# Six plain column blocks, late sums of squares, and new ranks and slacks for the list scheduler of a two-layer encoder

## The chip, the cores and the metric

The kernel runs on one core of a Trainium2 chip. The metric is the device time of one execution in microseconds (us). The core has a matrix engine (TensorE, PE; PEld is its weight load), VectorE (DVE), ScalarE (ACT), GpSimd (POOL), a queue (SP) that issues DMAs, an on-chip memory SBUF and accumulation banks PSUM.

## What is computed

Two layers of an encoder over 512 positions of width 1024, all in float32. Each layer:

```
h = rmsnorm(x, g_attn);  proj = h @ w_in
group A: windowed attention (8 q heads, 2 kv heads, dim 64, sinks)
group B: differential attention (4 heads): softmax 1 - lambda * softmax 2
x = x + concat(A, B) @ w_out
h = rmsnorm(x, g_ffn)
gate, val = split(h @ w_up)           # 22 column blocks of 128 each
gate = depthwise conv of width 3 over positions
x = x + (silu(gate) * val) @ w_down
```

## The kernel before

Every product is made of three float32r products of a high and a low part (hi*hi, hi*lo, lo*hi), so each weight tile `wr` that a DMA brings is split: ScalarE casts it to `wh`, VectorE (in some cases GpSimd) subtracts to get `wl`. The tiles `wr`, `wh` and `wl` have 2, 3 and 3 buffers.

**A layer** has a front and a mixer. The front is the first product `akv`/`aq`, seven projections `pj_...`, attention A (scores `sc_a`, softmax `so_a`, transposes `pt_a` into the one PSUM bank of tag `at`, their copies `p_a`, values `pv_a`), attention B (`sc_b`, `e_b`, transposes `wt_b`, values `yb`, their norm with `ss_yb`, `rr_yb`, `rt_yb`) and the output projection `wo` in three passes. The last pass adds its two halves of 256 positions to the residual `x`; after the second half the norm of the mixer is begun for each of the 8 row blocks k (`Norm.add`): ScalarE writes `nf_h` (x times the gain), VectorE `nf_l` (the rest). The squares (`Norm.squares`: `nf_q` on ScalarE, summed into `nf_sum` on VectorE) go to TensorE as `nf_ss`, then through GpSimd to the row factor `nf_r`, which TensorE spreads (`rps`) and ScalarE copies to `rb`. The factor multiplies the products afterwards, so the first products of the mixer need only `nf_h` and `nf_l`.

**The mixer** has 22 column blocks f. A plain block (`up_step`) is two products, gate and value, of 8 row blocks x 3 matmuls of 512 columns. A pair (`pair_step`, `up_pair`) makes two blocks together in a fast form with seven products of half size for each of gate and value (4 row blocks x 3 matmuls of 256 columns each). It needs sums of the weights (`ws`, four for each of gate and value, `w_sums`), splits of four weight tiles instead of two, sums of its inputs (`mixer_forms`: `fa`, `fb`, `fc`, `f`), and sums of its products (`dp`, `du`, `gp`). In a pair the last product T4 goes into the bank of T3, after VectorE has read T3 into `du` (`fourth`). With `PLAIN = 4`, blocks 0 to 3 are plain and 9 pairs follow. The down-projection `dn` of one part of blocks (`FF_PARTS`) stands between the pairs of the next. `gp` also is the padded gate, and `cv` its convolution.

**The order of all work is set when the program is built**, by a list scheduler (`Machine`). Each strand of work is a generator (a track) that yields one operation at a time, with a rank from the table `RK` (lower goes first). `Machine.run` takes for each engine the operations that could start within a hold (`HOLD`, 0.02 for PE) of the earliest, and of these the one of the lowest rank; it estimates when inputs are ready from modelled durations plus a slack per reading engine (`NEAR`, in us). Where an operation may go to VectorE or GpSimd (`either`), it takes the one that would end first, with `BIAS` added to VectorE:

```
q, op = min(((self.when(v), v) for v in (t[3] if isinstance(t[3], tuple) else (t[3],))),
            key=lambda v: self.begin(v[1], v[0]) + v[1].pitch + (BIAS if v[1].eng == "DVE" else 0))
```

The ranks that matter below: `nsq` (squares of the mixer's norm), `xl` (the adds of the last `wo` pass and the `Norm.add` behind them), `w` and `wf` (splits of weights), `sum` (`ws`), `hf` (forms), `sec` (`du`), `evac` (copies of projections out of PSUM), `a` and `b` (attention). The chip's engines each run their list in order; the estimates have no part in the run.

Of the kernel before, what the change touches and what calls it, by code (L numbers as in the profile page):

```python
# [14 lines left out]
ALU = mybir.AluOpType  # L15
# [3 lines left out]
S = 512  # L19
# [7 lines left out]
EPS = 1e-6  # L27
NEG = -1e30
FF_PARTS = ((0, 6), (6, 12), (12, 18), (18, 22))
PLAIN = 4  # L30
CHUNKS = ("akv", "aq0", "aq1", "bv0", "bk1", "bk0", "bq0", "bq1", "bv1")
CW = 256
RP = 4
SMP = 12
FIRST_TAGS = ("mm", "sc")
AQ_TAGS = ("mm", "sc")
HOLD = 0.1
SWITCH = {True: 0.2, False: 0.085}
NEAR = {"PE": 0.053, "POOL": 0.079, "DVE": 0.06, "ACT": 0.035}
BIAS = 0  # L40
SQ_FROM = 4
LO_CUT = 1
N_COL = NK + NK + 3 * NF + NF + 1
N_ROW = 4 * HD + 8 + 4 * HD


RK = {"w": (2, 45, 30), "qkb": (55, 18), "x": 33, "xl": 8, "a": 2, "b": 18, "evac": 49, "qka": 60, "kv": 45,
      "bn": 2, "nsq": 6, "av": -4, "bv": 4, "ch": 50, "add": 42, "sec": 1, "nxs": 42, "fin": 42, "sum": 25,
      "hf": 22, "wf": 36}


class Op:
# [101 lines left out]
class Machine:  # L154
# [52 lines left out]
    def when(self, op):  # L207
        t = self.free[op.eng]
        near = NEAR.get(op.eng, 0.035)
        for kind, items in (("r", op.reads), ("w", op.writes)):  # L210
# [50 lines left out]
    def run(self):  # L261
        while self.tracks:
            best = {}
            for t in list(self.tracks):
                while callable(t[3]) and t in self.tracks and t[3]():
                    self.step(t)
                if t not in self.tracks or callable(t[3]):
                    continue
                q, op = min(((self.when(v), v) for v in (t[3] if isinstance(t[3], tuple) else (t[3],))),
                            key=lambda v: self.begin(v[1], v[0]) + v[1].pitch + (BIAS if v[1].eng == "DVE" else 0))  # L270
                best.setdefault(op.eng, []).append((self.begin(op, q), t[0](), t[1], t, op, q))
# [5 lines left out]
            for eng, c in best.items():  # L277
                s0 = min(v[0] for v in c)
                hold = 0.02 if eng == "PE" else HOLD
                w = min((v for v in c if v[0] <= s0 + hold), key=lambda v: (v[1], v[2]))  # L280
# [21 lines left out]
def kernel(  # L302
# [20 lines left out]
    pe, dve, act, pool, sync = (Queue(e) for e in ("PE", "DVE", "ACT", "POOL", "SP"))  # L323
# [15 lines left out]
    def new(tag, name, shape=None, dtype=None):  # L339
        bufs, shp, dt = TAGS[tag]  # L340
        return m.got(tag, (ps if tag in BANKS else sb).tile(shape or shp, dtype or dt, tag=tag, bufs=bufs, name=name))
# [33 lines left out]
    def mixer_order():  # L375

        ups = [[(f, 1) for f in range(f0, min(f1, PLAIN))] + [(f, 2) for f in range(max(f0, PLAIN), f1, 2)]
               for f0, f1 in FF_PARTS]
        for f, n in ups[0]:
            yield "up", 0, f, n  # L380
        for pi in range(len(FF_PARTS)):
            after = ups[pi + 1] if pi + 1 < len(FF_PARTS) else []
            at = {NK * i // len(after): u for i, u in enumerate(after)}
            for d in range(NK):
                if d in at:
                    yield ("up", pi + 1, *at[d])
                yield "dn", pi, d, 0
# [26 lines left out]
    def w_rank():  # L414
        i = state["used"]
        if i < len(units) and units[i][2] in ("up", "pair", "sum", "rest", "down") and len(ready) > i:
            return RK["wf"]
        return RK["w"][min(len(ready) - i, 2)]

# [36 lines left out]
    def w_sums():  # L456
        either = lambda *a: tuple(e.tensor_tensor(out=a[0], in0=a[1], in1=a[2], op=a[3]) for e in (dve, pool))
        for i in range(len(units)):
            if units[i][2] != "pair":
                continue  # L460
            yield lambda: i in pairs
            ra, rb = pairs.pop(i)
            nh = units[i][1][0] // 2
            a11, a12, a21, a22 = ra.tile[:, :nh], ra.tile[:, nh:], rb.tile[:, :nh], rb.tile[:, nh:]
            new_t = lambda j, r: Shared("prob", new("prob", f"ws{i}_{j}", [P, 2 * nh, P], F32), r)
            yield m.room("prob")
            s14 = new_t(0, 1)
            yield either(s14.tile[:, :nh], a21, a22, ALU.add)
            yield m.room("prob")
            s32 = new_t(1, 2)  # L470
            yield either(s32.tile[:, nh:], s14.tile[:, :nh], a11, ALU.subtract)
            yield either(s14.tile[:, nh:], a12, s32.tile[:, nh:], ALU.subtract)
            s32.done()
            raws[i + 1] = s14
            yield either(s32.tile[:, :nh], a11, a21, ALU.subtract)
            raws[i + 2] = s32
            ra.done()
            raws[i + 3] = rb
# [55 lines left out]
    class Norm:  # L534
# [16 lines left out]
            m.flags.add(f"{self.name}{k}")  # L551

        def squares(self):
            eng = dve
            for k in range(NK):
                yield m.has(f"{self.name}{k}")
                if k == 0:
                    yield m.room("tab")
                    self.part = new("tab", f"{self.name}_sum", [P, S])
                    yield act.activation(self.part, x_sb[k], AF.Square)  # L560
                    continue
                yield m.room("tmp")
                sq = new("tmp", f"{self.name}_q{k}")
                yield act.activation(sq[:, :S], x_sb[k], AF.Square)
                yield eng.tensor_tensor(out=self.part, in0=self.part, in1=sq[:, :S], op=ALU.add)
                m.drop("tmp", sq)
            m.flags.add(f"{self.name}_sq")

# [21 lines left out]
    def loads():  # L590
# [11 lines left out]
        for f in (w_load, w_high, w_low):  # L602
            m.spawn(w_rank, f(4))
        m.spawn(lambda: RK["sum"], w_sums())
        yield lambda: len(his) >= 5
# [59 lines left out]
    def layer(l, norm):  # L665
# [73 lines left out]
        def qk_track(nm, views, gone, tp, tab, dst, rq, rank, is_kv=False):  # L739
            def go():  # L740
                yield m.has(f"{h_in.name}_r")
                yield m.room("rp", 2)
                raw = new("rp", f"raw_{nm}{l}_{tp}")
                sq_t = new("rp", f"sq_{nm}{l}_{tp}")
                for i in range(2):
                    yield act.activation(raw[:, i], views[i], AF.Copy,
                                         scale=h_in.r[:, 2 * tp + i:2 * tp + i + 1])
                    gone(i)
                m.spawn(rank, qk_out(nm, raw, sq_t, tp, tab, dst, rq, is_kv))
            m.spawn(RK["evac"], go())  # L750

# [78 lines left out]
        def first_done(banks, tp):  # L830
            left = [2, 2]

            def gone(i):
                left[i] -= 1
                if not left[i]:
                    m.drop(*banks[i][:2])
            qk_track("ka", [b[2][:, :CW] for b in banks], gone, tp, 1, [v.unsqueeze(1) for v in ka], None, RK["kv"], True)
            qk_track("qa0", [b[2][:, CW:] for b in banks], gone, tp, 0, qa[0], rqa_of(0, tp), RK["qka"])

# [688 lines left out]
        def ffn():  # L1528
            steps = list(mixer_order())
            b_st["rb_left"] = PLAIN + 1  # L1530
            mix["forms"] = 14
# [149 lines left out]
```

## Time and profile before

| | |
|---|---|
| runs without the profiler | 1184.47 us median of 3 (1183.8, 1184.47, 1187.16) |
| the profiled execution, its own time | 1185.19 us |
| its span, first to last instruction | 1183.1 us |
| mean granted clock of TensorE | 0.993 |
| busy: TensorE, VectorE, ScalarE, GpSimd | 98%, 83%, 56%, 17% of the span |
| fronts | 0 to about 236 us (layer 0), about 592 to 823 us (layer 1) |
| mixers | about 236 to 592 us and 823 to 1183 us |

The span is 2.1 us shorter than the execution's own time. Matmuls overlap, so TensorE's busy time says little of how dense it is; the distance from one matmul's start to the next does.

### The profile page before, as it was taken

How to read it: one execution, taken by the hardware profiler on the slowest of the kernel's cores; microseconds unless marked ns; L12 is line 12 of the kernel's file. 1: busy time of each engine (PE TensorE's matmuls, PEld its weight loads, DVE VectorE, ACT ScalarE, POOL GpSimd, SP SyncE). 2: the span in 40 equal slices, each digit the busy share in tenths (PEclk: the TensorE clock that was granted, in tenths of full speed). 3: DMA queues.
4: the chain of work that ended last, by engine and by line, in shares of the span. 5: the costliest groups of instructions: out<-in, count | busy, mean ns of one | idle time of the engine just before them, and what ended most of it. 6: DMA issues, size and time to landing. Idle time of an engine off the chain costs nothing.

```text
span 1183.1 us, 20177 instructions
## 1 busy us (share of the span) xinstructions
PE 1163.1 (98%) x7796; PEld 1053.0 (89%) x7796; DVE 981.9 (83%) x1797; ACT 663.2 (56%) x1187; POOL 202.3 (17%) x254
## 2 busy tenths in 40 slices
PE   9999999999999999999999989999999999999998
PEld 7999888978999999999889989888789999999997
DVE  6988899779998888887659888898799988888863
ACT  6779766455564454444537876665555544544441
POOL 2433721010100000000042556110111000000000
PEclk9999999989999999999999999999899999999999
DMA  6221111123223322332332121111232223233323
GB/s 233 66 72 55 54 55 36 54 72 107 68 99 112 111 99 99 112 125 71 107 118 73 37 71 37 55 54 54 71 124 61 96 88 112 98 112 103 121 81 116
DMA packets 33343, 103.12 MB, mean 87 GB/s; under 512 B 3936, under 2 KB 4192, under 8 KB 33248
## 3 DMA queue, kind: packets, MB, share of 16 engines
q1 hardware_dynamic: 33248, 101.84, 26.0%
q8 instruction: 61, 1.00, 0.4%
q14 instruction: 34, 0.28, 0.1%
HBM read 99.73 MB, written 2.10 MB: 86 GB/s over the span
## 4 chain that ended last, share of the span: by engine, by line
PE 79%; DVE 13%; ACT 5%; issue 2%; POOL 0%; DMA 0%; SPq 0%; DVEq 0%; ACTq 0%
PE up L258 32%; PE dn L258 20%; PE wo L258 6%; PE pj_bk L258 3%; PE pj_bv L258 2%; PE pj_akq L258 2%; PE pj_bq L258 2%; DVE wl L258 2%; PE yb L258 2%; PE sc_b L258 2%; PE pt_a L258 1%; PE pv_a L258 1%; PE sc_a L258 1%; PE wt_b L258 1%; ACT so_a L258 1%
## 5 line engine op out<-in xcount | busy, mean ns | idle before, releaser
L258 ACT CAST wh<-wr 128x1024 fp32r<-128x1024 f32 (+2 forms) x200 | 177.2, 887 | 158.9 <-PE up L258 41.3
L258 DVE TENSOR_TENSOR wl<-wr,wh 128x1024 fp32r<-128x1024 f32 (+2 forms) x193 | 196.7, 1020 | 62.9 <-ACT wh L258 62.7
L258 ACT CAST wh<-ws 128x1024 fp32r<-128x1024 f32 x72 | 75.4, 1048 | 109.2 <-DVE ws L258 46.1
L258 PE MATMUL up<-fc,wh 128*128 128x256 f32 x576 | 106.4, 285 | 1.8 <-DVE du L258 1.8
L258 PE MATMUL up<-fa,wh 128*128 128x256 f32 x576 | 107.0, 283 | 0.0
L258 PE MATMUL up<-fb,wh 128*128 128x256 f32 x576 | 105.6, 284 | 0.0
L258 PEld LDWEIGHTS up<-fc,wh 128*128 128x128 f32 x576 | 89.4, 191 | 2.6 <-ACT cv L258 2.1
L258 PEld LDWEIGHTS up<-fb,wh 128*128 128x128 f32 x576 | 89.8, 192 | 0.4 <-ACT dp L258 0.2
L258 PEld LDWEIGHTS up<-fa,wh 128*128 128x128 f32 x576 | 89.8, 192 | 0.1
L258 DVE TENSOR_TENSOR wl<-ws,wh 128x1024 fp32r<-128x1024 f32 x72 | 89.5, 1245 | 0.4 <-ACT wh L258 0.2
L258 PE MATMUL dn<-act,wh 128*128 128x512 f32 x288 | 88.9, 390 | 0.0
L258 PE MATMUL up<-fa,wl 128*128 128x256 f32 x288 | 81.7, 284 | 0.0
L258 PE MATMUL up<-fb,wl 128*128 128x256 f32 x288 | 81.5, 283 | 0.0
L258 PE MATMUL up<-fc,wl 128*128 128x256 f32 x288 | 81.4, 283 | 0.0
L258 PE MATMUL dn<-acth,wh 128*128 128x512 f32 x208 | 81.0, 389 | 0.0
L258 PE MATMUL dn<-actl,wh 128*128 128x512 f32 x208 | 81.0, 389 | 0.0
L258 PE MATMUL dn<-acth,wl 128*128 128x512 f32 x208 | 80.9, 389 | 0.0
L258 POOL TENSOR_TENSOR du<-du 128x256 f32<-128x256 f32 x12 | 8.9, 742 | 395.9 <-DVE du L258 395.9
L258 DVE TENSOR_TENSOR x<-x,dn 128x512 f32<-128x512 f32 x64 | 43.7, 682 | 32.8 <-PE dn L258 32.8
L258 DVE SCALAR_TENSOR_TENSOR cv<-gp,cols,cv 128x512 f32<-128x512 f32 x88 | 63.9, 745 | 0.0
L258 PEld LDWEIGHTS dn<-act,wh 128*128 128x128 f32 x288 | 53.3, 188 | 10.4
L258 ACT ACTIVATE e_b<-sc_b,mx_b,rqb 128x512 f32<-128x512 f32 x64 | 49.1, 776 | 14.6 <-DVE mx_b L258 14.6
(269 smaller groups left out, 3452.4 us busy)
## 6 DMA issues: line engine op xcount, KB each, us to landing
wr<-w_up SPq DMA_DIRECT2D x88, 512.0 KB, 4.5
wr<-w_down SPq DMA_DIRECT2D x48, 384.0 KB, 3.1
wr<-w_in SPq DMA_DIRECT2D x28, 512.0 KB, 3.5
wr<-w_out SPq DMA_DIRECT2D x16, 512.0 KB, 3.4
wr<-w_down SPq DMA_DIRECT2D x16, 256.0 KB, 2.6
x<-xT SPq DMA_DIRECT2D x8, 256.0 KB, 5.5
prob_f<-w_first SPq DMA_DIRECT2D x8, 256.0 KB, 5.6
wr<-w_first SPq DMA_DIRECT2D x4, 512.0 KB, 3.6
```

The lines of the kernel that those rows point to most:

```text
L258: getattr(self.raw[op.eng], op.name)(*op.args, **op.kw)
```

## The change

The number of plain blocks goes from 4 to 6, so each layer has 8 pairs instead of 9 and the first pair is blocks 6 and 7. The slack of TensorE's inputs goes from 0.053 to 0.15 us, that of ScalarE from 0.035 to 0.06, the hold of the other engines from 0.1 to 0.05, and `BIAS` from 0 to 0.3. Nearly all ranks change. The variable `eng` in `squares` is only renamed. No loop or formula of the computation is touched.

```diff
-PLAIN = 4
+PLAIN = 6
...
-HOLD = 0.1
+HOLD = 0.05
 SWITCH = {True: 0.2, False: 0.085}
-NEAR = {"PE": 0.053, "POOL": 0.079, "DVE": 0.06, "ACT": 0.035}
-BIAS = 0
+NEAR = {"PE": 0.15, "POOL": 0.079, "DVE": 0.06, "ACT": 0.06}
+BIAS = 0.3
...
-RK = {"w": (2, 45, 30), "qkb": (55, 18), "x": 33, "xl": 8, "a": 2, "b": 18, "evac": 49, "qka": 60, "kv": 45,
-      "bn": 2, "nsq": 6, "av": -4, "bv": 4, "ch": 50, "add": 42, "sec": 1, "nxs": 42, "fin": 42, "sum": 25,
-      "hf": 22, "wf": 36}
+RK = {"w": (2, 39, 1), "qkb": (55, 18), "x": 10, "xl": 28, "a": 12, "b": 18, "evac": 45, "qka": 400, "kv": 60,
+      "bn": 0, "nsq": 30, "av": -2, "bv": -2, "ch": 50, "add": 4, "sec": 400, "nxs": 18, "fin": 400, "sum": 2,
+      "hf": 10, "wf": 33}
```

**First place.** VectorE's order before, where layer 0's mixer begins: the last adds `x` of the output projection, the low parts `nf0_l2` to `nf0_l6` of the norm, and the running sum of squares `nf0_sum`.

```order
L258 SCALAR_TENSOR_TENSOR nf0_l2_3082<-x2_68,cols_75,nf0_h2_3064 128x512
L258 TENSOR_TENSOR wl27_3068<-wr27_2873,wh27_3052 128x1024
L258 SCALAR_TENSOR_TENSOR nf0_l3_3094<-x3_69,cols_75,nf0_h3_3078 128x512
L258 TENSOR_TENSOR nf0_sum_3044<-nf0_sum_3044,nf0_q2_3098 128x512
L258 SCALAR_TENSOR_TENSOR nf0_l4_3119<-x4_70,cols_75,nf0_h4_3085 128x512
L258 TENSOR_TENSOR nf0_sum_3044<-nf0_sum_3044,nf0_q3_3121 128x512
L258 SCALAR_TENSOR_TENSOR nf0_l5_3128<-x5_71,cols_75,nf0_h5_3091 128x512
L258 TENSOR_TENSOR nf0_sum_3044<-nf0_sum_3044,nf0_q4_3130 128x512
L258 TENSOR_TENSOR x6_72<-x6_72,wo0_2_1_6_3074 128x256
L258 TENSOR_TENSOR nf0_sum_3044<-nf0_sum_3044,nf0_q5_3137 128x512
L258 TENSOR_TENSOR x7_73<-x7_73,wo0_2_1_7_3087 128x256
L258 SCALAR_TENSOR_TENSOR nf0_l6_3146<-x6_72,cols_75,nf0_h6_3143 128x512
```

The same place in the changed kernel:

```order
L258 SCALAR_TENSOR_TENSOR nf0_l2_3062<-x2_68,cols_75,nf0_h2_3054 128x512
L258 TENSOR_TENSOR x4_70<-x4_70,wo0_2_1_4_3050 128x256
L258 TENSOR_TENSOR x5_71<-x5_71,wo0_2_1_5_3065 128x256
L258 SCALAR_TENSOR_TENSOR nf0_l3_3080<-x3_69,cols_75,nf0_h3_3070 128x512
L258 TENSOR_TENSOR wl27_3090<-wr27_2859,wh27_3051 128x1024
L258 TENSOR_TENSOR x6_72<-x6_72,wo0_2_1_6_3076 128x256
L258 TENSOR_TENSOR x7_73<-x7_73,wo0_2_1_7_3087 128x256
L258 SCALAR_TENSOR_TENSOR nf0_l4_3112<-x4_70,cols_75,nf0_h4_3085 128x512
L258 SCALAR_TENSOR_TENSOR nf0_l5_3120<-x5_71,cols_75,nf0_h5_3093 128x512
L258 SCALAR_TENSOR_TENSOR nf0_l6_3128<-x6_72,cols_75,nf0_h6_3117 128x512
L258 SCALAR_TENSOR_TENSOR nf0_l7_3131<-x7_73,cols_75,nf0_h7_3122 128x512
L258 TENSOR_TENSOR nf0_sum_3044<-nf0_sum_3044,nf0_q1_3059 128x512
```

Before, six of the seven adds into `nf0_sum` stand ahead of `nf0_l7`; now all seven stand behind it. On TensorE `nf0_ss`, which reads the sum, moves from behind 24 of the mixer's matmuls to behind 54, and `rps0` still stands 9 matmuls behind `nf0_ss`.

**Second place.** TensorE's order before, in attention A of layer 1: the second and third block of transposes for the query block 1 of head pair 1 (`pt_a1_1_1_1`, `pt_a1_1_1_2`).

```order
L258 MATMUL pj1_bq0_1_8132<-wh151_7968,na1_l7_6886 128x256
L258 MATMUL pt_a1_1_1_1_8289<-ident_74,so_a1_1_1_0_0_7988 128x128
L258 MATMUL pt_a1_1_1_1_8289<-ident_74,so_a1_1_1_1_0_7990 128x128
L258 MATMUL pt_a1_1_1_1_8289<-ident_74,so_a1_1_1_0_1_7989 128x128
L258 MATMUL pt_a1_1_1_1_8289<-ident_74,so_a1_1_1_1_1_7991 128x128
L258 MATMUL pt_a1_1_1_2_8308<-ident_74,so_a1_1_1_0_0_7988 128x128
L258 MATMUL pt_a1_1_1_2_8308<-ident_74,so_a1_1_1_1_0_7990 128x128
L258 MATMUL pt_a1_1_1_2_8308<-ident_74,so_a1_1_1_0_1_7989 128x128
```

The same place in the changed kernel, up to the last of the transposes of the second block and the matmuls behind it:

```order
L258 MATMUL pt_a1_1_1_1_8136<-ident_74,so_a1_1_1_1_1_7859 128x128
L258 MATMUL pj1_bq0_1_8080<-wh147_7902,na1_h4_6645 128x256
L258 MATMUL pj1_bq0_1_8080<-wl147_7937,na1_h4_6645 128x256
L258 MATMUL pj1_bq0_1_8080<-wh147_7902,na1_l4_6653 128x256
L258 MATMUL pj1_bq0_1_8080<-wh147_7902,na1_h5_6677 128x256
L258 MATMUL pj1_bq0_1_8080<-wl147_7937,na1_h5_6677 128x256
L258 MATMUL pj1_bq0_1_8080<-wh147_7902,na1_l5_6685 128x256
```

Twelve matmuls of the projection now stand between the two blocks of transposes, six of which are shown; before there was none. Between the first and the second block 18 stand instead of 9. In layer 0 the same block of transposes is now 12 behind the second instead of 15, and in the next query block, where before none stood, there are 15. Further on, behind the last `yb` product of a front and before the first `wo` matmul that needs its norm, there were 21 matmuls of 512 and 48 of 256 columns in layer 0, and 9 and 48 in layer 1; now there are 37 of 256 in each.

**Third place.** GpSimd's order in the changed kernel, in the second part of blocks of layer 0's mixer: sums of weights (`ws`), edges and sums of the padded gate (`gp`), and one sum of products (`du`).

```order
L258 TENSOR_TENSOR ws59_0_4274<-wr59_1_4265 128x512
L258 TENSOR_TENSOR ws63_0_4363<-wr63_1_4318 128x512
L258 MEMSET gp0_10_4390 128x1 x2
L258 MEMSET gp0_11_4391 128x1 x2
L258 TENSOR_TENSOR gp0_11_4391<-du0_10_0_4387 128x256
L258 TENSOR_TENSOR du0_10_1_4510<-du0_10_1_4510 128x256
L258 TENSOR_TENSOR ws70_0_4627<-wr70_1_4618 128x512
```

Before, no `ws` stood on GpSimd, 4 of the 18 `gp<-du` and 12 of the 18 `du<-du` did, and 7 of the `wl`. Now 30 of 128 `ws`, all 16 `gp<-du`, all 16 `du<-du`, 4 of 8 sums `ht` of the forms and one `wl` do.

## Rows read from the trace of the kernel before

**Rows 1.** The page's line of busy time by engine (us, share of the span, instructions), and its line of the granted clock in 40 equal slices (tenths of full speed).

```profile
PE 1163.1 (98%) x7796; PEld 1053.0 (89%) x7796; DVE 981.9 (83%) x1797; ACT 663.2 (56%) x1187; POOL 202.3 (17%) x254
...
PEclk9999999989999999999999999999899999999999
```

**Rows 2.** Busy time of each engine in three stretches of the mixers (from:to, length, then the busy us of each engine with its instructions, the granted clock, the share of the DMA engines and GB/s).

```profile
262.00:300.00 38.00, 37.11 (x204) 32.34 (x203) 37.23 (x62) 22.49 (x35) 4.66 (x11) 1.00 0.32 105
300.00:554.00 254.00, 253.99 (x1790) 239.48 (x1789) 219.08 (x342) 127.37 (x185) 12.02 (x41) 1.00 0.29 97
...
887.00:1141.00 254.00, 253.96 (x1786) 239.04 (x1785) 218.37 (x341) 126.92 (x184) 11.81 (x41) 1.00 0.29 96
```

**Rows 3.** The chain that ended last, in order of time, three pieces in the mixer of layer 0 (start us, us, engine, tile, matmuls).

```profile
318.65 11.90 PE up L258 x96
...
432.01 20.19 PE up L258 x168
452.20 12.27 PE dn L258 x54
```

**Rows 4.** TensorE in order of time where the mixer of layer 0 begins (start us, us, engine, line, operation, output<-inputs, shapes, count, and in brackets the idle time before and what ended it).

```profile
236.20 0.40 PE L258 MATMUL up<-nf_h,wh 128*128 128x512 f32 x1
...
242.76 0.50 PE L258 MATMUL up<-nf_h,wh 128*128 128x512 f32 x1 [0.95 <-ACT nf_h L258]
...
244.86 0.79 PE L258 MATMUL up<-nf_l,wh 128*128 128x512 f32 x1 [0.30 <-DVE nf_l L258]
...
245.88 1.70 PE L258 MATMUL nf_ss<-unit,nf_sum 128*128 128x1 f32 x8
247.44 0.77 PE L258 MATMUL up<-nf_h,wh 128*128 128x512 f32 x1
...
251.43 1.12 PE L258 MATMUL rps<-ident,nf_r 128*128 128x128 f32 x8
252.31 0.48 PE L258 MATMUL up<-nf_h,wh 128*128 128x512 f32 x1
...
255.84 0.39 PE L258 MATMUL up<-nf_h,wh 128*128 128x512 f32 x1
...
261.28 0.39 PE L258 MATMUL up<-nf_h,wh 128*128 128x512 f32 x1
```

**Rows 5.** The same columns as rows 2, over three short stretches (the granted clock is the number after POOL's bracket).

```profile
244.75:251.57 6.82, 6.71 (x20) 5.64 (x21) 3.10 (x5) 1.05 (x1) 2.08 (x5) 0.50 0.44 145
...
831.84:838.67 6.83, 6.83 (x22) 5.73 (x23) 2.84 (x4) 1.05 (x1) 2.08 (x5) 0.50 0.48 151
...
702.13:705.55 3.42, 3.42 (x22) 3.19 (x22) 2.40 (x6) 2.34 (x6) 3.42 (x3) 0.50 0.00 0
```

**Rows 6.** ScalarE and then VectorE in order of time at the same place.

```profile
231.82 1.44 ACT L258 ACTIVATE nf_h<-x,cols 128x512 fp32r<-128x512 f32 x2 [6.51 <-DVE x L258]
...
232.58 1.47 DVE L258 SCALAR_TENSOR_TENSOR nf_l<-x,cols,nf_h 128x512 fp32r<-128x512 f32 x2
...
239.00 0.75 DVE L258 SCALAR_TENSOR_TENSOR nf_l<-x,cols,nf_h 128x512 fp32r<-128x512 f32 x1
...
242.47 0.41 DVE L258 TENSOR_TENSOR x<-x,wo 128x256 f32<-128x256 f32 x1
...
244.06 0.74 DVE L258 SCALAR_TENSOR_TENSOR nf_l<-x,cols,nf_h 128x512 fp32r<-128x512 f32 x1
```

**Rows 7.** A group of VectorE's instructions over the whole span (output<-inputs, shapes, count, busy us, mean ns of one, idle before).

```profile
L258 DVE TENSOR_TENSOR nf_sum<-nf_sum,nf_q 128x512 f32<-128x512 f32 x14 | 9.6, 686 | 0.0
```

**Rows 8.** TensorE in the first pair of each layer's mixer.

```profile
298.25 0.47 PE L258 MATMUL up<-fc,wh 128*128 128x256 f32 x2 [0.89 <-DVE du L258]
...
885.14 0.47 PE L258 MATMUL up<-fc,wh 128*128 128x256 f32 x2 [0.88 <-DVE du L258]
```

**Rows 9.** TensorE in the attention stretch of layer 0 and, after the cut, of layer 1.

```profile
122.95 0.66 PE L258 MATMUL pt_a<-ident,so_a 128*128 128x128 f32 x4
125.01 0.66 PE L258 MATMUL pt_a<-ident,so_a 128*128 128x128 f32 x4 [1.40 <-DVE p_a L258]
...
127.30 0.38 PE L258 MATMUL pj_bq<-wh,na_h 128*128 128x256 f32 x1 [0.69 <-ACT raw_bq L258]
...
696.61 0.63 PE L258 MATMUL pt_a<-ident,so_a 128*128 128x128 f32 x4 [0.53 <-DVE ng_a L258]
...
699.59 0.66 PE L258 MATMUL pt_a<-ident,so_a 128*128 128x128 f32 x4 [1.28 <-DVE p_a L258]
701.88 0.91 PE L258 MATMUL pt_a<-ident,so_a 128*128 128x128 f32 x4 [1.63 <-DVE p_a L258]
```

**Rows 10.** GpSimd and then VectorE in order of time in the first pair of layer 0.

```profile
310.46 1.55 POOL L258 TENSOR_TENSOR cv<-cv,rb 128x512 f32<-128x512 f32 x1 [0.49 <-ACT cv L258]
...
309.63 1.22 DVE L258 TENSOR_TENSOR wl<-ws,wh 128x1024 fp32r<-128x1024 f32 x1
...
311.43 1.66 DVE L258 TENSOR_TENSOR wl<-ws,wh 128x1024 fp32r<-128x1024 f32 x1
```

**Rows 11.** Groups of instructions over the whole span, two of GpSimd and one of VectorE (columns as in rows 7).

```profile
L258 POOL TENSOR_TENSOR raw_bk<-raw_bk,sq_bk 128x512 f32<-128x512 f32 x8 | 10.3, 1290 | 0.6
...
L258 POOL TENSOR_TENSOR gp<-du 128x256 f32<-128x256 f32 x4 | 9.3, 2327 | 56.3 <-DVE du L258 56.3
...
L258 DVE TENSOR_TENSOR ws<-wr 128x512 f32<-128x512 f32 x36 | 24.6, 684 | 0.1
```

More of the change, by code (lines that the diff above doesn't have):

```diff
@@ L553, in squares @@
         def squares(self):
-            eng = dve
             for k in range(NK):
@@ L564, in squares @@
                 yield act.activation(sq[:, :S], x_sb[k], AF.Square)
-                yield eng.tensor_tensor(out=self.part, in0=self.part, in1=sq[:, :S], op=ALU.add)
+                yield dve.tensor_tensor(out=self.part, in0=self.part, in1=sq[:, :S], op=ALU.add)
                 m.drop("tmp", sq)
```

## The prediction

> **What bounds the kernel now.** I read the page first. TensorE is busy 98% of the span at nearly full clock [rows 1], but busy says little for overlapping matmuls, so I read distances between starts. In the dense mixer 168 matmuls of 256 columns (one pair) take 20.19 us, 0.120 us each, and 54 of 512 columns 12.27 us, 0.227 us each [rows 3]. TensorE is busy in 253.99 of 254 us there, in both layers, while VectorE is busy in 219 [rows 2]. So the dense mixer stands at TensorE's own pace. Gains can only come from fewer matmul columns, which this change does not bring, or from the places where TensorE waits or runs at half clock. The list of waits and the windows of the clock lead to three:
>
> - The start of each mixer. 48 matmuls of 512 columns and 16 small ones take from 236.20 to 255.84, 19.64 us [rows 4]; the next 24, undisturbed, take 5.44 [rows 4]. At that pace 48 need 10.88. TensorE first waits for `nf_h` and `nf_l`, and from 244.75 it is granted 0.50, 1.2 of 2.4 GHz, for 6.82 us [rows 5]. Layer 1 shows the same 0.50 for 6.83 us [rows 5].
> - The first pair of each mixer: 0.89 and 0.88 us for `du` [rows 8].
> - Attention A: blocks of transposes that follow each other with nothing between, 1.40, 1.28 and 1.63 us of wait for the copy out of the one bank [rows 9], and after the last two 0.50 of the clock for 3.42 us [rows 5].
>
> **The change part by part.** The sum is made against the profiled execution, 1185.19 us, of which the span is 1183.1 and 2.1 lie around it; it lies 0.7 us above the median of the runs.
>
> *Two more plain blocks in place of a pair, each layer.* A pair is 168 matmuls of 256 columns, 20.19 us [rows 3]. Two plain blocks are four products of 24 matmuls of 512 columns, 5.44 us each [rows 4], 21.76 us. That costs 1.57 us a layer, **+3.1** together, in a stretch where nothing else is waited for. It also takes work off the other engines: eight `ws` sums a layer (0.684 us each [rows 11]), and of the splits of weights two of 1024 and two of 512 columns. That is worth nothing by itself, since VectorE has 35 us of idle time in the 254 us of dense mixer [rows 2]; that idle time is the cover for the last item below.
>
> *Late sums of squares.* Between the first `nf_l` at 232.58 and the last, which ends at 244.80 [rows 6], VectorE also does six `nf_sum` adds of 0.686 us [rows 7]. Now they come behind. I chain the new order of VectorE (first place in the change) with the durations of the rows: two `nf_l` 1.47 [rows 6], an `x` 0.41 [rows 6], a `wl` 1.22 [rows 10]. The adds and subtractions from `nf0_l0` at 232.58 are then 8 `nf_l` at 0.74, 6 `x` and one `wl`, 5.9 + 2.5 + 1.2 = 9.6 us, so the last `nf_l` ends near 242.2, 2.6 us earlier. TensorE needs the low part of row block k at 236.20 + 0.23 + 0.68 k. The fifth, k = 4, then comes at 240.0 instead of the wanted 239.15: one wait of 0.9, and some 0.2 later. Before, TensorE's waits in this stretch are 19.64 less 10.88, less 1.7 for the small matmuls (8 at about 0.11 each for `nf_ss`, and 0.88 for `rps` from 251.43 to 252.31 [rows 4]), less 3.4 for the half clock: 3.65 us. Now 1.1, and the sum of squares ends later: seven adds and two `wl` behind 242.2 give 249.4 to 249.5, when TensorE, 54 matmuls of 0.227 and 1.1 of waits after 236.20, comes to `nf_ss`; I add 0.5 for it. `rps` still stands only 9 matmuls behind, 2.0 us, although a `wl` and about 2 us of GpSimd's `nf_r` [rows 5] lie between, the `wl` mostly beside `nf_ss`; I add 0.7. Whether the clock falls again after these shorter waits no row shows; the nearest are the stretch of layer 0's attention, where waits of 1.40 and 0.69 us two microseconds apart [rows 9] left the clock at full, against 1.28 and 1.63 close together, which it followed down. I take full. That is 2.3 us of waits in place of 7.05 of waits and clock: 4.75 a layer, **-9.5** together. The ends: -14.1 without any wait, -2.7 if the clock falls as before.
>
> *First pair later.* `du` is late because VectorE works almost without a gap through the forms, the splits and the first plain blocks, 37.23 us of the 38 from 262 to 300 [rows 2]. The first pair now starts two plain blocks, 21.8 us, later, for which VectorE has about 12 us more work (4 `wl`, and per block a gate product, two convolution steps, a value product and a low part of 0.7 each). So about 10 us of cover arise where there was none, and the 0.89 and 0.88 go: **-1.8**; 0 if the low rank of `sec` puts `du` behind other work.
>
> *More slack for TensorE's inputs.* In both layers filler matmuls now separate the transposes (second place). From one block to the next with nothing between are 2.06 and 2.29 us [rows 9]; the 12 or 15 matmuls of 0.120 [rows 3] now in between use 1.44 or 1.80 of it, and the four transposes themselves part of the rest, so 0.2 to 0.4 remains at most. The 1.40, 1.28 and 1.63 become 0, 0.2 and 0.4, the 3.42 us of half clock end, 1.7: -5.4. Filler used here is missing later. Behind the last `yb` only 37 matmuls now cover the chain of the last heads' norm (end of the second place). I allow 0.5 us of new waits a layer: from below nothing, from above the 1.63 of the longest wait in such a chain; nearer nothing, because 37 matmuls of 0.120, 4.4 us, still cover it. **-4.4**, ends -7 (the waits of 0.69 and 0.53 go as well) and 0.
>
> *Work from VectorE to GpSimd.* 30 weight sums of 512 columns and 12 more gate sums go to GpSimd. A sum of this size takes 1.290 us there and 0.684 on VectorE, and `gp<-du` took 2.327 there [rows 11]. They are off the path as long as VectorE's 35 us a layer cover them: 0. What they take from VectorE: beside a GpSimd sum of 1.55 us, a subtraction that otherwise takes 1.22 took 1.66 [rows 10]. Some 50 more GpSimd sums at 0.44 are 22 us over both mixers, about what the 30 sums that leave VectorE save it (30 x 0.684 = 20.5). Without the cover the cost would be that of a rival below.
>
> The Trainium skill, SBUF — State Buffer, section "SBUF: two separate sides", holds that VectorE and GpSimd share a port pair as an exclusive lock, and whoever starts first blocks the other for its whole instruction. Rows 10 agree in kind (1.66 against 1.22); an estimate by that page, 50 sums of up to 1.29 us, would be 64 us of VectorE, nearly the 70 us of idle time; by that rule the rival on the weights below would come out.
>
> The sum: +3.1 - 9.5 - 1.8 - 4.4 = -12.6, that is 1185.2 - 12.6 = 1172.6 us of the profiled execution, and about **1172 us** for a median.
>
> **The rivals.**
>
> *The clock still falls at the start of the mixer.* The waits shrink from 3.65 to 2.3 us but do not vanish, and 0.50 stays for 6.8 us a layer. Each costs 3.4, together 6.8: 1179. For it: full clock is lost three times in the trace, each time among waits of about a microsecond. Against: the waits now stand apart.
>
> *Nearly all waits go.* With the favourable ends -14.1 and -7 the sum is 1185.2 + 3.1 - 14.1 - 1.8 - 7 = 1165.4. For it: the new order has filler at each place; against: the first wait on `nf_l` follows from durations.
>
> *GpSimd's sums hold up the weights, slower.* Place: the 32 half pairs of the two mixers. A `ws` on GpSimd is late, VectorE stands in its queue at the next `ws`, which reads it; `wl` stands behind, and TensorE for `wl`. In the trace the stretch with GpSimd sums beside a pair is 318.65, 96 matmuls in 11.90 us where 0.120 each give 11.54 [rows 3]: 0.36 lost. At 0.36 in each of 32, the sum is +11.5 - 12.6: 1184, no change. From 0.5 us it decides for slower; at 0.7, 1195. Against it: three pieces of a pair are ready ahead by the buffers, and VectorE has less to do.
>
> *It does nothing.* The plan's new slack moves waits instead of removing them: the front's gains cancel (+4.4) and the norm's shrink to -2.7: 1184.
>
> **How the numbers follow.** Forecast, 1166 to 1177: 0.62. Nearly all waits gone, under 1166: 0.12. Clock still falls, 1177 to 1181: 0.12. No change, within 0.3% (3.6 us, about what three runs of this kernel can tell from nothing), 1181 to 1188: 0.07. Slower: 0.07. Faster by over 0.3% is 0.62 + 0.12 + 0.12 = 0.86. The range 1163 to 1182 leaves out some 0.04 below and 0.12 above.
>
> **What would show it.** The mixers' first 48 matmuls in about 15 us with full clock; no wait for `du` in the first pair; no block of transposes waiting over 0.5 us in attention A and full clock there; dense mixers at 20.2 us a pair, unchanged, with eight pairs; TensorE waiting there for `wl` or `ws` would show the rival. Wrong I would be if VectorE, with GpSimd at its port, fell behind in the pairs, or if waits moved to the end of the fronts, before the last `wo` pass.

## The result and the profile after

The changed kernel takes 1170.39 us (median of 4 runs, 1169.66 to 1170.7); the kernel before, beside it, 1184.13 (4 runs). The ratio is 0.9882, 95% interval 0.9863 to 0.9901: 13.7 us faster. The profiled execution took 1170.7 us with a span of 1168.9, against 1183.1.

The page after, its busy time and its granted clock in 40 slices (against [rows 1]):

```profile
PE 1155.1 (99%) x7652; PEld 1042.7 (89%) x7652; DVE 966.8 (83%) x1709; ACT 652.1 (56%) x1169; POOL 246.8 (21%) x302
...
PEclk9999999999999999999999999999999999999999
```

The two slices that show 8 before show 9 now (0.9 or more), and the mean granted clock is 1.00 for 0.993. TensorE in order of time where the mixer of layer 0 begins (against [rows 4]):

```profile
236.85 0.40 PE L258 MATMUL up<-nf_h,wh 128*128 128x512 f32 x1
...
247.92 0.39 PE L258 MATMUL up<-nf_h,wh 128*128 128x512 f32 x1
...
249.28 0.95 PE L258 MATMUL nf_ss<-unit,nf_sum 128*128 128x1 f32 x8
250.09 0.49 PE L258 MATMUL up<-nf_h,wh 128*128 128x512 f32 x1
...
252.27 1.05 PE L258 MATMUL rps<-ident,nf_r 128*128 128x128 f32 x8
...
255.22 0.39 PE L258 MATMUL up<-nf_h,wh 128*128 128x512 f32 x1
```

No row has a wait. The first 48 matmuls take 11.07 us (236.85 to 247.92) where 10.88 is the undisturbed pace; the first 72 with all 16 small ones take 18.37 us (to 255.22), where before they took 25.08 (236.20 to 261.28 [rows 4]). That is 6.7 us; layer 1 gains as much (by the table below, 52.3 and 21.8 for two more plain blocks against 67.3).

VectorE there (against the second half of [rows 6]): the last four low parts run together, the sums of squares stand behind.

```profile
233.22 0.75 DVE L258 SCALAR_TENSOR_TENSOR nf_l<-x,cols,nf_h 128x512 fp32r<-128x512 f32 x1
...
237.20 1.22 DVE L258 TENSOR_TENSOR wl<-wr,wh 128x1024 fp32r<-128x1024 f32 x1
238.34 0.75 DVE L258 TENSOR_TENSOR x<-x,wo 128x256 f32<-128x256 f32 x2
239.00 2.74 DVE L258 SCALAR_TENSOR_TENSOR nf_l<-x,cols,nf_h 128x512 fp32r<-128x512 f32 x4
...
245.12 3.88 DVE L258 TENSOR_TENSOR nf_sum<-nf_sum,nf_q 128x512 f32<-128x512 f32 x5
```

The chain in the dense mixer is as before (against [rows 3]), a pair and 54 matmuls of `dn`. Then come the two pieces in layer 1 between which the chain leaves TensorE; the second begins behind a wait for `wl`, shown further below:

```profile
332.68 20.21 PE up L258 x168
352.89 12.27 PE dn L258 x54
...
975.94 15.89 PE up L258 x132
...
1006.83 18.80 PE up L258 x154
```

The list of TensorE's waits over the whole span (us in total, times, longest):

```profile
PE pt_a L258 <- DVE p_a L258: 3.2, 4, 1.2
PE ss_yb L258 <- DVE wl_b L258: 1.5, 2, 0.7
...
PE pj_bk L258 <- DVE wl L258: 0.9, 2, 0.5
PE up L258 <- DVE wl L258: 0.8, 1, 0.8
PE wt_b L258 <- DVE bq0l L258: 0.8, 2, 0.4
```

`nf_l`, `nf_h` and `du` are gone from it, but attention A still waits for `p_a`, and the smaller waits for `wl`, `wl_b` of `ss_yb` and `bq0l` are new. The parts, from the first matmul of each in the traces (us; "plain" to the first matmul of the first pair, "pairs" to the next front or the last matmul):

| kernel | front 0 | plain 0 | pairs 0 | front 1 | plain 1 | pairs 1 |
|---|---|---|---|---|---|---|
| before | 229.5 | 52.3 | 303.2 | 231.4 | 52.3 | 303.6 |
| changed | 230.0 | 67.3 | 281.7 | 229.3 | 67.3 | 282.3 |
| late squares alone | 229.7 | 47.2 | 312.7 | 232.0 | 47.2 | 312.3 |
| six plain alone | 229.7 | 71.4 | 281.9 | 230.9 | 73.6 | 281.9 |
| BIAS alone | 229.5 | 52.4 | 302.6 | 229.6 | 52.1 | 302.8 |
| other ranks and slacks alone | 229.8 | 52.8 | 319.7 | 237.3 | 53.3 | 319.6 |
| slack alone | 241.9 | 53.1 | 303.5 | 231.2 | 49.6 | 303.1 |
| late squares, six plain | 229.4 | 68.9 | 281.8 | 232.0 | 68.9 | 281.5 |
| changed, early squares | 230.7 | 75.1 | 282.7 | 229.3 | 75.1 | 282.0 |
| changed, four plain | 230.9 | 45.6 | 326.0 | 230.6 | 45.5 | 324.6 |
| changed, four plain, early du | 229.8 | 45.6 | 311.3 | 229.6 | 45.5 | 311.7 |
| changed, BIAS 0 | 230.4 | 67.3 | 281.6 | 232.9 | 67.3 | 281.2 |
| changed, old slack | 236.0 | 67.3 | 281.9 | 241.9 | 67.3 | 281.2 |
| changed, sums on VectorE | 229.9 | 67.3 | 281.5 | 229.2 | 67.3 | 281.4 |

Before against changed: the fronts 1.6 us, the mixers 12.8, nearly all of it from their starts.

### The profile page after: what moved, and what is told of

Same layout as the page of the kernel before. It is cut to its first block, busy times and chain, and to the rows that moved or that the text cites. A ratio compares the mean times of both kernels' runs of the same rounds, so it can differ in the third digit from the quotient of the medians.

```text
span 1168.9 us, 19845 instructions
## 1 busy us (share of the span) xinstructions
PE 1155.1 (99%) x7652; PEld 1042.7 (89%) x7652; DVE 966.8 (83%) x1709; ACT 652.1 (56%) x1169; POOL 246.8 (21%) x302
## 4 chain that ended last, share of the span: by engine, by line
PE 84%; DVE 8%; ACT 5%; issue 1%; DMA 1%; POOL 0%; SPq 0%; DVEq 0%; ACTq 0%
PE up L258 38%; PE dn L258 20%; PE wo L258 7%; PE pj_bk L258 3%; PE pj_akq L258 3%; PE yb L258 2%; PE pj_bq L258 2%; PE pj_bv L258 2%; PE sc_b L258 1%; DVE so_a L258 1%; PE pv_a L258 1%; DVE wl L258 1%; PE pt_a L258 1%; ACT e_b L258 1%; ACT so_a L258 1%
## 5 line engine op out<-in xcount | busy, mean ns | idle before, releaser
L258 DVE TENSOR_TENSOR wl<-wr,wh 128x1024 fp32r<-128x1024 f32 (+2 forms) x199 | 211.4, 1064 | 64.8 <-ACT wh L258 64.7
L258 PE MATMUL up<-fa,wh 128*128 128x256 f32 x512 | 95.0, 283 | 0.0
L258 PE MATMUL up<-fc,wh 128*128 128x256 f32 x512 | 94.2, 284 | 0.0
L258 PE MATMUL up<-fb,wh 128*128 128x256 f32 x512 | 93.5, 283 | 0.0
L258 PEld LDWEIGHTS up<-fb,wh 128*128 128x128 f32 x512 | 79.9, 192 | 0.0
L258 PEld LDWEIGHTS up<-fa,wh 128*128 128x128 f32 x512 | 79.8, 192 | 0.0
L258 PEld LDWEIGHTS up<-fc,wh 128*128 128x128 f32 x512 | 79.6, 192 | 0.0
L258 PE MATMUL up<-nf_h,wh 128*128 128x512 f32 x192 | 75.2, 392 | 0.0
L258 PE MATMUL up<-nf_l,wh 128*128 128x512 f32 x192 | 75.0, 390 | 0.0
L258 PE MATMUL up<-nf_h,wl 128*128 128x512 f32 x192 | 74.8, 389 | 0.0
```

The costliest lines, as they stand in the source:

```text
L258: getattr(self.raw[op.eng], op.name)(*op.args, **op.kw)
```

## The experiments

All ratios are to the kernel before, with 95% intervals.

### Parts of the change alone

```diff
-      "bn": 2, "nsq": 6, ...
+      "bn": 2, "nsq": 30, ...
```

> The kernel before with one number changed, the rank of the squares of the mixer's norm (6 to 30). TensorE's order stays the same but for the 16 small matmuls nf_ss. Theory (what the trace of the changed kernel shows at its mixer starts, where the first 48 matmuls took 11.1 us beside 17.2): the late squares alone remove the waits and the half clock, 6 to 6.7 us a layer, so the time falls by 12 to 13.5 us, to about 1171.5. The forecast's own term: -9.5 us, 1175. Rival, the gain at the mixer's start needs the two further plain blocks or the other ranks: under 5 us, 1180 or more. The first pair's wait for du of 0.9 us should stay.

Measured: 1190.44 us, 1.0052 (1.0038 to 1.0067): slower by 6.2 us. The start ran at full clock and gained 5.1 us a layer (47.2 for 52.3), a little less than expected, and the pairs lost more, 9.5 and 8.6 us. TensorE's waits in this kernel:

```profile
PE up L258 <- DVE dp L258: 4.9, 2, 2.4
...
PE up L258 <- ACT dp L258: 3.1, 2, 1.7
PE up L258 <- ACT f L258: 2.3, 2, 1.1
...
PE up L258 <- DVE f L258: 0.9, 2, 0.5
PE up L258 <- DVE fa L258: 0.7, 1, 0.7
```

And two stretches at its first pair (columns as [rows 2]):

```profile
283.19:292.40 9.21, 5.22 (x34) 4.42 (x33) 9.20 (x16) 4.99 (x9) 1.97 (x5) 0.96 0.00 0
...
291.80:295.30 3.50, 3.50 (x19) 3.50 (x18) 2.10 (x5) 0.89 (x2) 0.00 (x0) 0.52 0.00 0
```

Before this pair can run, VectorE has to end the forms, sums and splits; here it is busy in 9.20 of 9.21 us while TensorE has 5.22. The late squares take no work off VectorE. TensorE reaches the pair 5.3 us earlier (283.19 for 288.48) and VectorE, already 0.9 us late for `du` before [rows 8], is late by all of it; then the clock falls too. Neither theory had this: both expected only the 0.9 to stay.

```diff
-PLAIN = 4
+PLAIN = 6
```

> The kernel before with PLAIN = 6 alone. Forecast's terms: two plain blocks for a pair cost +1.6 us a layer, and the first pair's wait for du (0.89 and 0.88 us) goes: +3.1 - 1.8 = +1.3 us, 1185.5 to 1186. The stretch from the first up matmul to the first pair grows by 21.8 us, and everything behind shrinks by 20.2 and 0.9. Rival, the wait for du goes elsewhere: +3.1.

Measured: 1184.74 us, 1.0012 (1.0000 to 1.0023), 1.4 us by the ratio: as forecast. The pairs are 21.3 us shorter in layer 0, 20.19 of it the pair, most of the rest the wait for `du`, of which 0.2 stays. The profiled execution, 1182.21 us, is the fastest of the eleven. Its clock did not fall at the start of layer 0 (last section), so the two layers part what the start loses against the changed kernel's 67.3 us: 4.1 in layer 0 (71.4) by waits alone, 6.3 in layer 1 (73.6) by waits and clock.

Both together:

```diff
-PLAIN = 4
+PLAIN = 6
...
-      "bn": 2, "nsq": 6, ...
+      "bn": 2, "nsq": 30, ...
```

> The kernel before with the late rank of the squares (30) and PLAIN = 6 together; nothing else. Coupling theory: the late squares bring 5.1 us a layer at the mixer's start, as alone, and the two further plain blocks give VectorE the 10 us that it lacked before the first pair (alone, it was some 8.5 us late there in each layer), so -10.3 + 1.3 = -9 us, near 1175. Rival 1, the lateness before the first pair stays although it starts 21.8 us later: 1190 or more. Rival 2, the gain at the start needs the other ranks too: 1180 or more.

Measured: 1174.42 us, 0.9914 (0.9897 to 0.9931), -10.2 us. Alone the two numbers cost 6.2 and 1.4. The coupling theory holds: pairs of 281.8 and 281.5 us, no wait in them. The two plain blocks are the condition of the gain, not a price beside it. Some 4 us are left to the rest of the change: 1.6 in each mixer's start (68.9 for 67.3), where waits for `nf_h` and `nf_l` of up to 0.34 us remain, and 2.7 in front 1, whose clock is at 0.50 from 695.7 to 702.5 us here. Which of the other ranks brings the 1.6, no run separates.

```diff
-BIAS = 0
+BIAS = 0.3
```

> The kernel before with BIAS = 0.3 alone: 29 sums of weights, 14 of the gate, 8 of the convolution and 4 of products go from VectorE to GpSimd in the two mixers; TensorE's order of matmuls is the same to the last row. Forecast's term: nothing, within 1.5 us, since VectorE has 35 us of idle time in each dense mixer. Rival, GpSimd's sums hold up the weights: 0.36 us or more in each of the half pairs that have one, 5 to 12 us slower, and TensorE's list of waits shows wl or ws in the dense mixers.

Measured: 1181.04 us, 0.9971 (0.9959 to 0.9982): a gain that neither had. In the profiled execution the mixers give 0.4 and 1.1 us (of the 1.8 us of waits for `du` 0.3 stay). Front 1 gives 1.8, and there every engine has the instructions of the kernel before in the same order, and the waits of attention A are the same. This kernel's clock behind them (against the third row of [rows 5]):

```profile
699.50:706.00 6.50, 4.87 (x43) 4.37 (x44) 4.63 (x13) 5.93 (x15) 6.34 (x5) 1.00 0.23 81
```

So that 1.8 is the clock not falling in this execution, not GpSimd's. How the other six executions divide their gain is not shown.

```diff
-NEAR = {"PE": 0.053, ...
+NEAR = {"PE": 0.15, ...
```

> The kernel before with the slack of TensorE's inputs alone at 0.15 us. Forecast's term, if the slack is what puts filler between the transposes and filler alone removes the waits: -3 to -5 us. Theory after seeing the changed kernel: filler between two blocks of transposes does not shorten the copy out of the one bank, which stands on ScalarE and VectorE behind casts and subtractions of the filler's own weights (1.04 and 1.22 us each); waits move: within 2 us of the kernel before.

Measured: 1195.83 us, 1.0094 (1.0076 to 1.0112). Both expectations failed: front 0 is 12.4 us longer, front 1 0.2 shorter. TensorE's waits of front 0 (7 to 249 us):

```profile
PE pt_a L258 <- DVE p_a L258: 4.7, 5, 2.2
PE tr_bq L258 <- DVE mx_b L258: 1.5, 1, 1.5
```

The other ranks and slacks alone, that is the changed kernel with three numbers put back:

```diff
-PLAIN = 6
+PLAIN = 4
...
-BIAS = 0.3
+BIAS = 0
...
-      "bn": 0, "nsq": 30, ...
+      "bn": 0, "nsq": 6, ...
```

> The changed kernel with three numbers put back: PLAIN = 4, BIAS = 0 and the rank of the squares 6. What is left of the change is the slacks, the hold and all other ranks. Layer 0's front has then the same order as in the changed kernel on every engine. Forecast's term for the fronts: -4.4 us. What the changed kernel's trace shows of its fronts: +0.5 in layer 0 and -2.1 in layer 1, so -1.6 us, near 1182.5. Rival, these ranks also change the start of the mixers (sums of weights and forms ahead of the squares): up to 5 us more or less at 236 to 300 us.

Measured: 1228.81 us, 1.0369 (1.0350 to 1.0387), 44 us slower, far outside what was expected. Front 0 is the changed kernel's (229.8 us). Front 1 has another order than the changed kernel's and is 8.0 us longer than it (237.3 for 229.3), 4.2 of them one wait of `pj_bv` for `raw_qa`. The pairs are 16 us longer than before in each layer, on waits for `du`:

```profile
PE up L258 <- DVE du L258: 23.5, 9, 4.3
```

### Parts of the change undone

```diff
-      "bn": 0, "nsq": 30, ...
+      "bn": 0, "nsq": 6, ...
```

> The changed kernel with the rank of the squares back at 6; both fronts keep the changed kernel's order. Theory: each mixer's start gets its waits and half clock back; its first 288 matmuls take 67.3 us in the changed kernel and 71.4 to 73.6 in the kernel before with six plain blocks, and 7.2 more than their due in the run with the other ranks alone: +5 to +7 us a layer, 1180 to 1185. Rival, the other ranks hold the gain without the late squares: under 1175.

Measured: 1186.62 us, 1.0017 (1.0008 to 1.0026), 16.2 us behind the changed kernel: 7.8 us in each of the two starts, and the rest in the pairs and front 0. It is a little more than expected; waits and clock both have a part in it. The start of layer 0 here, in two pieces:

```profile
240.00:246.00 6.00, 3.39 (x10) 1.64 (x10) 6.00 (x11) 4.12 (x8) 0.00 (x0) 1.00 0.36 96
...
246.00:253.00 7.00, 6.70 (x22) 5.25 (x21) 2.42 (x4) 1.04 (x1) 2.08 (x5) 0.56 0.37 132
```

TensorE is busy in 3.39 of 6 us while VectorE is in all 6; then the clock falls.

```diff
-PLAIN = 6
+PLAIN = 4
```

> The changed kernel with PLAIN = 4. By the forecast's separate terms: -3.1 + 1.8, so 1169, no worse. Coupling theory: the first pair of each mixer starts 21.8 us earlier and VectorE is late for it again, 5 to 12 us a layer of waits on f, fa, dp or du, so 1180 to 1192.

Measured: 1214.78 us, 1.0246 (1.0223 to 1.0269): 44 us worse than the changed kernel, where the forecast's separate terms say 1 better, and worse than the 1192 that the coupling theory allowed. The waits, and the longest in the order of time:

```profile
PE up L258 <- DVE du L258: 17.7, 6, 7.9
PE up L258 <- ACT dp L258: 6.9, 4, 2.6
PE up L258 <- ACT f L258: 3.2, 2, 1.6
...
320.68 0.77 PE L258 MATMUL up<-fc,wh 128*128 128x256 f32 x2 [7.88 <-DVE du L258]
```

Then, beside it, the rank of `du` back:

```diff
-PLAIN = 6
+PLAIN = 4
...
-      ... "sec": 400, ...
+      ... "sec": 1, ...
```

> The changed kernel with PLAIN = 4 and the rank of du (sec) back at 1, TensorE's order that of the run with PLAIN = 4. Theory: of the 44 us that PLAIN = 4 cost there, the 17.7 us of waits for du and what the clock lost with them come from du standing last in VectorE's order, so 1186 to 1196. Rival, VectorE is simply short of time with four plain blocks, whatever the rank: waits move from du to wl, ws or dp, and 1205 or more.

Measured: 1186.61 us, 1.0019 (1.0008 to 1.0030). TensorE's order is the same, `du` is gone from its waits and 28 us with it:

```profile
PE up L258 <- ACT dp L258: 4.9, 2, 2.5
PE up L258 <- ACT f L258: 3.2, 2, 1.6
...
PE up L258 <- DVE f L258: 2.5, 2, 1.2
```

What stays is 8.2 and 8.1 us in the pairs of the two layers against the kernel before, about what the late squares alone cost there (9.5 and 8.6), with waits for `dp` and `f` as there. Ranking `du` last is free only while VectorE is ahead.

```diff
-BIAS = 0.3
+BIAS = 0
```

> The changed kernel with BIAS = 0: 30 sums of weights and 15 of the gate go back from GpSimd to VectorE. Forecast's term: nothing, within 1.5 us, near 1170. What the same number did alone on the kernel before: -2.8 us, so 1173 without it. Rival, only GpSimd's help keeps du and dp in time under the new ranks (sums first, du last): waits for du as in the run with the other ranks alone, 10 us or more, 1180 to 1200.

Measured: 1173.78 us, 0.9908 (0.9891 to 0.9925). The mixers are no longer (348.9 and 348.5 us, changed 349.0 and 349.7). So GpSimd's help brings nothing in the mixers. The 3.4 us are in front 1 (232.9 for 229.3), which the scheduler orders in another way. The next run leaves the order of the fronts as it is.

```diff
-        either = lambda *a: tuple(e.tensor_tensor(...) for e in (dve, pool))
+        either = lambda *a: tuple(e.tensor_tensor(...) for e in (dve,))
```

(in `w_sums` alone)

> The changed kernel with the 30 sums of weights kept on VectorE, the rest of BIAS left in force; TensorE's order is that of the changed kernel to the last row, so the fronts keep their time (unlike in the run with BIAS = 0, whose second front had another order). Theory: in the mixers GpSimd's sums bring nothing and cost the one wait for wl at 1005.7 us, so the mixer of layer 1 gets 0.8 to 1.1 us shorter (348.5 against 349.65 us), that of layer 0 stays: 1169.3 to 1169.7. Rival, VectorE has no room for the sums: waits for du or wl in the dense mixers, 2 us or more slower.

Measured: 1169.45 us, 0.9873 (0.9856 to 0.9889), as expected: pairs of layer 1 281.4 for 282.3 us, all else within 0.2. The median is 0.9 us under the changed kernel's; the intervals overlap, so it is the equal order and the one vanished wait that speak for it. That wait, in the changed kernel:

```profile
1006.83 0.39 PE L258 MATMUL up<-fa,wl 128*128 128x256 f32 x1 [0.82 <-DVE wl L258]
```

VectorE's splits of the sums, first in the changed kernel, then with the sums on VectorE, and that kernel's busy line:

```profile
L258 DVE TENSOR_TENSOR wl<-ws,wh 128x1024 fp32r<-128x1024 f32 x64 | 86.9, 1359 | 1.9
```

```profile
L258 DVE TENSOR_TENSOR wl<-ws,wh 128x1024 fp32r<-128x1024 f32 x64 | 79.8, 1250 | 1.9 <-ACT wh L258 0.5
...
PE 1154.2 (99%) x7652; PEld 1042.1 (89%) x7652; DVE 963.1 (83%) x1739; ACT 652.5 (56%) x1169; POOL 206.0 (18%) x272
```

VectorE does 30 sums more and is busy 3.7 us less.

```diff
-NEAR = {"PE": 0.15, ...
+NEAR = {"PE": 0.053, ...
```

> The changed kernel with the slack of TensorE's inputs back at 0.053 us. Forecast: the slack spreads the transposes, so both fronts lose 2 to 3 us without it, 1175. Theory after the run with the slack alone (layer 0's front 12.4 us slower, layer 1's 0.2 faster): slack and ranks place the filler together, and no front is better for one of them; within 3 us of 1170 if the new ranks carry the fronts, 1180 or more if they need the slack.

Measured: 1189.1 us, 1.0036 (1.0022 to 1.0050). Fronts 6.0 and 12.6 us longer, mixers as in the changed kernel. The longest wait of front 1:

```profile
703.02 1.08 PE L258 MATMUL pt_a<-ident,so_a 128*128 128x128 f32 x4 [4.43 <-DVE bk0l L258]
```

Of slack and ranks, either one alone makes a front up to 12 us worse; in the changed kernel both together end 0.5 us above and 2.1 below where the fronts were before. That is no property of slack and ranks alone: in the run with the other ranks and slacks, both are in force, and front 1, ordered in another way, is 5.9 us longer than before. Why the changed kernel's order fits is not shown.

## Why the prediction was right, by its own steps

The forecast was 1172 us; 1170.4 came, by the spans -14.2 where the sum has -12.6. The sum is better than its terms (last point).

- **Two plain blocks (+3.1) and the first pair (-1.8)**: right in size, alone (+1.4) and here: a pair is still 20.21 us. But the step "about 10 us of cover arise where there was none" set this cover against 0.9 us of `du`. It is needed for the late squares: without it they lose 6.2 us, with it they bring the time from 1.4 us above the kernel before to 10.2 below. The forecast read in [rows 2] that VectorE sets the first pair (37.23 of 38 us) and still took a gain of TensorE ahead of that pair as a gain of the whole.
- **Late squares (-9.5)**: mechanism right, mis-sized: -13.4. The first 72 matmuls at 0.2267 us are 16.3 and the small ones 1.6, so 0.4 us is lost where the forecast left 2.3. It chained durations end to end (`nf_l` 0.74, `x` 0.41, `wl` 1.22); in the rows the next instruction starts earlier, four `nf_l` in 2.74 us, 0.66 each. The last `nf_l` ends 4.9 us after the first matmul, not 6.0, and the wait of 0.9 for the fifth never comes. The Trainium skill, Vector Engine (DVE) Microarchitecture Reference, section "5.2 Measured stream behaviour on trn2 (trn3 not measured)", gives 1.0417 ns a column and some 75 ns an instruction between queued ones, an estimate of 0.61 us for 512 columns, 0.34 for 256 and 1.14 for 1024; the starts of this trace agree within 0.05: 0.66 from `nf_l` to `nf_l`, 0.33 from `x` to `x` and to `nf_l`, 1.14 from `wl` to `x`. The five `nf_sum`, each of which adds to the result of the one before, are 0.80 apart. The 0.5 and 0.7 for `nf_ss` and `rps` did not come either: the sums end at 249.0, `nf_ss` starts at 249.28.
- **The fronts (-4.4)**: wrong, -1.6: +0.5 in layer 0, -2.1 in layer 1, of which 1.7 is the clock. Of the three waits for `p_a` in [rows 9], 1.40 and 1.28 are gone, as forecast; 1.63 is still 1.22, layer 0 has a new one of 1.23 where nothing was waited for, and two of 0.4 are new. The step that failed is that the filler matmuls "now in between use 1.44 or 1.80 of it": it took the 2.06 and 2.29 us from block to block as fixed. The place of the 1.63, in layer 1, on TensorE, ScalarE and VectorE of the changed kernel, then on ScalarE of the kernel before:

```profile
691.04 0.60 PE L258 MATMUL pt_a<-ident,so_a 128*128 128x128 f32 x4
...
694.29 0.65 PE L258 MATMUL pt_a<-ident,so_a 128*128 128x128 f32 x4 [1.22 <-DVE p_a L258]
...
691.33 1.04 ACT L258 CAST wh<-wr 128x1024 fp32r<-128x1024 f32 x1
692.27 0.59 ACT L258 CAST p_a<-pt_a 128x512 fp32r<-128x512 f32 x1
...
692.40 1.23 DVE L258 TENSOR_TENSOR wl<-wr,wh 128x1024 fp32r<-128x1024 f32 x1 [0.56 <-ACT wh L258]
693.54 0.69 DVE L258 TENSOR_TENSOR p_a<-pt_a,p_a 128x512 fp32r<-128x512 f32 x1
```

```profile
700.53 0.57 ACT L258 CAST p_a<-pt_a 128x512 fp32r<-128x512 f32 x1
...
701.10 1.04 ACT L258 CAST wh<-wr 128x1024 fp32r<-128x1024 f32 x1
```

A cast of a weight stands ahead of `p_a` on ScalarE, its subtraction ahead of `p_a` on VectorE; before, the cast stood behind. From block to block are 3.25 us instead of 2.29: the filler is used up and 1.22 is waited all the same. The new wait of layer 0 (112.72 to 115.97) has the same order. The allowance of 0.5 a layer for new waits was too small as well (`ss_yb` 1.5, `pj_bk` 0.9, `wt_b` 0.8 in two layers).
- **GpSimd (0)**: nearly: +0.9, the single wait for `wl`; the rival of late weights exists at one place, not 32. The price of a GpSimd sum was too low: 30 of them cost VectorE 20.5 + 3.7 = 24.2 us, 0.81 each where the forecast took 0.44. By the Trainium skill, SBUF — State Buffer, section "SBUF: two separate sides", a GpSimd instruction that reads SBUF and starts first blocks a VectorE instruction with two SBUF inputs for its whole length; with such a one always beside it, the 1.29 us of each of the 30 would be lost, an estimate of 39 us. The runs lie between that and the 13 us of the forecast's 0.44.
- **The rivals**: the clock does not fall at any mixer start with late squares. "Nearly all waits go" came true for the mixers, "it does nothing" nearly so for the fronts.
- **The sum** is close in part by luck. The late squares were 3.9 us too small and the fronts 2.8 too large, which nearly cancel. Against GpSimd's +0.9 stand some 1.4 us that are in no term: the pairs are 21.5 and 21.3 us shorter, the second with the 0.8 of `wl` in it, where a pair and the wait for `du` make 21.1. Why is not shown.

That the late squares only work with the plain blocks, and the new ranks only with the new slack, was in no step. Without the late squares, the six plain blocks or the slack, this change is 16 to 44 us slower than with them.

## What to carry to other kernels

Before adding up gains ahead of a point, ask which engine sets the time at that point: a gain of another engine is paid back there as a wait unless slack is made first. Chain a queue by the distance from start to start, not by durations. Filler between two steps of a chain does not make the steps shorter; look which casts and subtractions stand ahead of the chain's own copy before counting it as cover.

## What the runs showed of the hardware

The same waits do not always take the clock down. With BIAS alone and with late squares alone, front 1 has the matmuls of the kernel before in the same order and the same waits for `p_a`, 1.28 to 1.29 and 1.63 to 1.64 us. Behind them the grant fell to 0.50 (1.2 of 2.4 GHz) for 3.42 us before [rows 5], stayed at 1.00 with BIAS alone (the row above), and fell for twice as long with late squares alone:

```profile
704.70:711.50 6.80, 5.67 (x30) 5.22 (x31) 5.86 (x9) 3.81 (x9) 6.07 (x4) 0.50 0.14 56
```

At the start of mixers with early squares it fell in 10 of 12 (two in each of six kernels), with late squares, whose waits are at most 0.34 us, in none of 16 (two in each of eight). The two exceptions have waits like the others; six plain alone, layer 0 (no fall) and layer 1:

```profile
244.90:251.40 6.50, 6.39 (x34) 5.09 (x35) 3.71 (x6) 1.63 (x2) 2.08 (x5) 1.00 0.48 156
...
829.00:835.50 6.50, 6.50 (x21) 5.40 (x21) 3.12 (x5) 1.04 (x1) 2.08 (x5) 0.53 0.42 129
```

What decides it among equal waits stays open. A term for lost clock that is read from one execution, as the forecast's 1.7 in front 1, can thus come out 0 or 3.4.
